# Moving sums to GpSimd and re-ordering the v stage of a hybrid RG-LRU and gated-MLP block on Trainium2

## The chip, the cores and the metric

The kernel runs on one core of one Trainium2 chip. The metric is the device time of one execution in microseconds. Five engines matter: TensorE (PE) multiplies matrices, VectorE (DVE), ScalarE (ACT) and GpSimd (POOL) work elementwise, and SyncE (SP) issues nearly all DMAs. Each engine runs its own instructions in order and waits on semaphores for the others.

## What is computed

One decoder block on x of 1024 tokens by 1024 channels, float32. The part that matters here is the first half, cut from the reference:

```
h = rms_norm(x, norm_mix_g)
rnn_x, rnn_gate, sgu_u, sgu_v, gate_a, gate_b = split(h @ w_in)
y_a = gelu(rnn_gate) * rg_lru(conv(rnn_x))        # decays use softplus(-rg_lambda)
v = layer_norm(gelu(sgu_v))                       # over 1024 channels, per token
mixed = einsum(tril(w_s), v) + b_s                # within chunks of 128 tokens, 8 groups
y_b = gelu(sgu_u) * mixed
merged = sigmoid(gate_a) * (y_a @ w_proj_a) + sigmoid(gate_b) * (y_b @ w_proj_b)
x = x + merged @ w_out
```

A SwiGLU channel mixer and a final RMSNorm follow. The change does not touch them.

## The kernel before

**Precision.** Each float32 operand is split into a high half, rounded on ACT, and a low half, subtracted on DVE (`split`, L91 to L94). A product is three matmuls: high by high, high by low, low by high (`mm3`, L96 to L99). For weights the pair of halves is made by `split_w`.

**The v stage** (pool `phv`, from L462). Tokens are rows here, in eight tiles t of 128. A first pass computes the first 512 channels of v for all tiles (product pv0, weight wv0), a second pass the other 512 (pv1, weight wv1; the loop at L708). After a tile's second half its statistics are complete: `v_stats` (gelu, bn_stats, bn_aggr), `v_norm` (the scale, by `rstd_early`, a chain of tiny instructions of one or two columns; tiles 1 and 2, 3 and 4, 5 and 6 share one chain), `v_centre` (four ACT instructions for a pair of tiles). One or two tiles later `v_split` makes the halves vn of v times its scale, ACT the high and DVE the low one, `v_mix` multiplies them on PE with the masked w_s (product mx), ACT copies one part (tile mt) and `v_mixed` adds the other on DVE and stores the sum to `mix_d`. The iteration of tile t mixes tile t - 2.

**Left operands.** From the u pair on, the input projections are done as 2x2 Strassen-Winograd products, seven instead of eight: M1 to M7 with left operands A11, A12, S4, A22, S1, S2, S3 (`LEFT`). They are made from the normalized x of the two halves of tokens F[0] and F[1]. `scale_x` normalizes a piece on DVE; `sums(i)` and `sum_s4(i)` (L548 to L555) make S1 to S4 in place, for the two halves i of the channels; `part` splits one half of an operand. The right operands need differences of weight blocks: `sums13` and `sum2` (L194 to L205).

**The order of the work.** Everything from L564 to the end of the u pair's first products (L787) stands in a hand-written order: within `tc.manual_schedule` each of the five engines issues its instructions in the order of the program text. Work behind it is ordered by the framework and may be issued between these instructions. Weights go through one queue of loads and splits: `weight` splits what a product needs and `ahead` more entries, `pump` splits up to a given entry. In the u pair (u0 and u1, order M1, M2, M5, M6, M3, M7, M4), `head` issues the next product, and `take` the evacuations that were postponed.

**Buffers.** vn has two, mt four, and S1's sums one (tag `shift`), so the sums of half 1 wait until the split of S1's half 0 has been done. The PSUM has eight banks.

**Recurrence constants.** softplus of lam is made after the u pair: lam is loaded by SP, ACT does Abs and Exp, and DVE does 17 instructions on 128x8 (L876 to L892).

## Time and profile before

| | |
|---|---|
| median of three runs | 1421.23 us (1419.32 to 1421.56) |
| the profiled execution | 1423.84 us |
| its span, first to last instruction | 1422.1 us |
| PE busy | 1399.9 us, 98% |
| PE weight loads busy | 1152.5 us, 81% |
| DVE busy | 1099.4 us, 77% |
| ACT busy | 793.3 us, 56% |
| POOL busy | 75.0 us, 5% |
| mean granted PE clock over the span | 0.996 |

All times within the execution are counted from the start of the span. The profiled execution took 1.7 us more than its span. Busy shares are means over stages with different limits. Matmuls are pipelined, so a PE that is always busy is not shown to be at its peak. In a timeline row the number in brackets is the idle time of that engine just before the instruction, with what ended it. PEclk is the clock that was granted to TensorE, as a share of its full 2.4 GHz.

The v stage's second pass runs from about 54 to 111 us, the u pair's products from 114 to 164 us, and the channel mixer, the only place where POOL does sums in this kernel, from about 800 to 1210 us.

### The profile page before, as it was taken

The page shows a single profiled execution, that of the slowest core. Times are in us where ns is not written, and L with a number is a line of the kernel's source. Part 1 is how long each engine was busy: PE and PEld are TensorE (multiplying, and loading weights), DVE is VectorE, ACT ScalarE, POOL GpSimd, SP SyncE. Part 2 cuts the span into 40 slices and gives each one's busy share as a digit, 9 for nine tenths or more (in the row PEclk, how much of TensorE's full clock was granted, in tenths as well). Part 3 has the DMA queues.
Part 4 walks back from the last instruction along what each step waited for, and adds up shares of the span by engine and source line. Part 5 has one row for each costly group of instructions (what it writes and reads, how often), then busy time and mean ns, then how long its engine had stood idle before and what let it go on. Part 6 is the DMA issues. An engine that isn't in the chain of part 4 may idle for free.

```text
span 1422.1 us, 17200 instructions
## 1 busy us (share of the span) xinstructions
PE 1399.9 (98%) x6216; PEld 1152.5 (81%) x6216; DVE 1099.4 (77%) x1807; ACT 793.3 (56%) x1320; POOL 75.0 (5%) x59
## 2 busy tenths in 40 slices
PE   9999999999999999999999999999999999999997
PEld 7877787788888887888888788888888888888886
DVE  6988999988888877788756976666666664697585
ACT  8567688888889865453543543333333333444454
POOL 0000000000000000000000021111111111000000
PEclk9999999999999999999999999999999999999999
DMA  9323645533333388683611133332232226852342
GB/s 322 138 60 101 196 169 171 175 125 104 116 108 114 104 303 320 236 322 127 230 60 45 74 112 112 111 112 91 102 112 112 111 85 256 331 191 85 112 141 81
DMA packets 72197, 212.45 MB, mean 149 GB/s; under 512 B 6448, under 2 KB 20784, under 8 KB 59568
## 3 DMA queue, kind: packets, MB, share of 16 engines
q1 hardware_dynamic: 71968, 211.32, 41.7%
q8 instruction: 48, 0.79, 0.2%
q14 instruction: 37, 0.30, 0.1%
q10 hardware_dynamic: 144, 0.04, 0.0%
HBM read 148.68 MB, written 62.65 MB: 149 GB/s over the span
## 4 chain that ended last, share of the span: by engine, by line
PE 74%; DVE 13%; ACT 8%; DMA 2%; issue 2%; SPq 0%; POOL 0%; DVEq 0%; ACTq 0%; POOLq 0%
PE f_p L97 10%; PE f_p L99 10%; PE f_p L98 10%; PE d_M L99 5%; PE d_M L97 5%; PE d_M L98 5%; PE g_p L98 2%; PE g_p L97 2%; PE g_p L99 2%; PE pb_p L97 2%; PE pb_p L99 2%; PE pb_p L98 2%; PE po L99 2%; PE po L97 2%; PE po L98 2%
## 5 line engine op out<-in xcount | busy, mean ns | idle before, releaser
L93 ACT ACTIVATE dl_M<-wraw 128x512 fp32r<-128x512 f32 x77 | 48.6, 631 | 104.9 <-PE d_M L99 92.3
L98 PE MATMUL d_M<-d_M,dl_M 128*128 128x512 f32 x264 | 102.8, 389 | 0.0
L97 PE MATMUL d_M<-d_M,dl_M 128*128 128x512 f32 x264 | 102.7, 389 | 0.0
L99 PE MATMUL d_M<-d_M,dl_M 128*128 128x512 f32 x264 | 102.7, 389 | 0.0
L93 ACT ACTIVATE f_t<-wraw 128x512 fp32r<-128x512 f32 x88 | 55.2, 630 | 84.1 <-PE f_p L99 64.1
L94 DVE TENSOR_TENSOR dl_M<-wraw,dl_M 128x512 fp32r<-128x512 f32 x77 | 54.0, 701 | 51.6 <-ACT dl_M L93 51.3
L94 DVE TENSOR_TENSOR f_t<-wraw,f_t 128x512 fp32r<-128x512 f32 x88 | 70.8, 806 | 23.4 <-ACT f_t L93 22.4
L97 PE MATMUL f_p<-f_S,f_t 128*128 128x512 f32 x176 | 68.6, 390 | 0.3 <-ACT f_t L93 0.3
L97 PE MATMUL f_p<-m,f_b 128*128 128x512 f32 x176 | 68.6, 390 | 0.0
L98 PE MATMUL f_p<-f_S,f_t 128*128 128x512 f32 x176 | 68.5, 389 | 0.0
L99 PE MATMUL f_p<-m,f_b 128*128 128x512 f32 x176 | 68.5, 389 | 0.0
L98 PE MATMUL f_p<-m,f_t 128*128 128x512 f32 x176 | 68.5, 389 | 0.0
L99 PE MATMUL f_p<-m,f_t 128*128 128x512 f32 x176 | 68.5, 389 | 0.0
L98 PE MATMUL f_p<-m,f_b 128*128 128x512 f32 x176 | 68.5, 389 | 0.0
L99 PE MATMUL f_p<-f_S,f_t 128*128 128x512 f32 x176 | 68.4, 390 | 0.0
L97 PE MATMUL f_p<-m,f_t 128*128 128x512 f32 x176 | 68.3, 389 | 0.0
L94 DVE TENSOR_TENSOR f_b<-wraw,f_b 128x512 fp32r<-128x512 f32 x66 | 47.2, 719 | 15.6 <-ACT f_b L93 14.9
L93 ACT ACTIVATE f_b<-wraw 128x512 fp32r<-128x512 f32 x66 | 40.9, 625 | 32.4 <-PE f_p L99 29.9
L98 PEld LDWEIGHTS d_M<-d_M,dl_M 128*128 128x128 f32 x264 | 49.6, 188 | 10.5 <-DVE d_M L94 0.2
L99 PEld LDWEIGHTS d_M<-d_M,dl_M 128*128 128x128 f32 x264 | 49.5, 188 | 10.3
L97 PEld LDWEIGHTS d_M<-d_M,dl_M 128*128 128x128 f32 x264 | 49.5, 188 | 10.2
L198 DVE TENSOR_TENSOR wraw<-wraw 128x512 f32<-128x512 f32 x50 | 53.0, 1060 | 1.1
(506 smaller groups left out, 4212.9 us busy)
## 6 DMA issues: line engine op xcount, KB each, us to landing
wraw<-in_w_gu_dram SPq DMA_DIRECT2D x22, 1024.0 KB, 4.9
wd<-in_w_down_dram SPq DMA_DIRECT2D x11, 1024.0 KB, 9.6
wraw<-in_w_r_dram SPq DMA_DIRECT2D x8, 1024.0 KB, 7.0
wraw<-in_w_g_dram SPq DMA_DIRECT2D x8, 1024.0 KB, 5.0
wraw<-ffs_d SPq DMA_DIRECT2D x8, 1024.0 KB, 5.0
wraw<-ffa_d SPq DMA_DIRECT2D x6, 1024.0 KB, 6.1
xn<-in_x_dram SPq DMA_DIRECT2D x8, 512.0 KB, 9.3
wraw<-in_w_u_dram SPq DMA_DIRECT2D x4, 1024.0 KB, 5.1
```

The source lines that it names most:

```text
L93: act.activation(hi, src, AF.Copy)
L94: return (eng or dve).tensor_sub(lo, src, hi.bitcast(F32))
L97: pe.matmul(o, lh, rh, start=start, stop=False, **kw)
L98: pe.matmul(o, lh, rl, start=False, stop=False, **kw)
L99: pe.matmul(o, ll, rh, start=False, stop=stop, **kw)
L198: dve.tensor_sub(raw[:, 0], raw[:, 2], raw[:, 0])
```

## The change

`sums` and `sum_s4` go from DVE to POOL, and so do `sums13` and `sum2` for u0 and u1 (the split of b22 inside `sum2` stays on ACT and DVE). The parts of the left operands move: A11's two halves to tiles 0 and 1, the first sums to tile 1, A12 to tile 5, S1's second half to tile 6. `v_mixed` becomes `mix_out(t, q)`, with one tile and one store for two mixing products; for the last two tiles it takes the places of v. In tile 7's iteration the first u weight is split, tile 5 is mixed and tile 6's vn made ahead of tile 7's statistics. In the u pair nothing is split ahead by the queue itself, but by explicit `pump` calls; the S3 and A22 parts and M3 move into the hand-written order. The constants of the recurrence are computed near the start: lam is loaded from ACT's queue, Abs and Exp are ACT's first instructions, and DVE's part stands before the first `x_rms`.

```diff
--- before.py
+++ after.py
@@ -191,18 +191,18 @@
     NORMED = ("M1", "M2", "M6", "M5", "M7", "M3", "M4")
     cur, postponed = {"misc": None, "defer": False}, []
 
-    def sums13(name, raw):
+    def sums13(name, raw, eng=dve):
 
         if (name, "t1") not in ready:
             ready[(name, "t1")] = True
-            dve.tensor_sub(raw[:, 0], raw[:, 2], raw[:, 0])
-            dve.tensor_sub(raw[:, 2], raw[:, 3], raw[:, 2])
-
-    def sum2(name, raw):
+            eng.tensor_sub(raw[:, 0], raw[:, 2], raw[:, 0])
+            eng.tensor_sub(raw[:, 2], raw[:, 3], raw[:, 2])
+
+    def sum2(name, raw, eng=dve):
 
         if (name, "b22") not in ready:
             ready[(name, "b22")] = split_w(raw[:, 3], f"{name}_b22")
-            dve.tensor_sub(raw[:, 3], raw[:, 3], raw[:, 0])
+            eng.tensor_sub(raw[:, 3], raw[:, 3], raw[:, 0])
 
     def plan(names, srcs, order=STEADY):
         lds = [new_load(s) for s in srcs]
@@ -374,7 +374,28 @@
     ident = const.tile([P, P], F32, name="ident")
     dve.memset(eps_t, EPS)
     make_identity(nc, ident)
-    act.activation(small.tile([P, 1], F32, name="warm", bufs=1), eps_t, AF.Gelu_apprx_tanh)
+    lam = const.tile([P, 8], F32, name="lam")
+    lam_c = const.tile([P, 2, 8], F32, name="lam_c")
+    act.dma_start(pv, a["pv"])
+    act.dma_start(lam, a["lam"])
+
+    def recurrence_constants(wk):
+
+
+        sp = {n: wk.tile([P, 8], F32, name=f"sp_{n}") for n in ("z", "z2", "p")}
+        e = lam_c[:, 0]
+        dve.tensor_scalar(sp["z"], e, 2.0, None, ALU.add)
+        dve.reciprocal(sp["z"], sp["z"])
+        dve.tensor_mul(sp["z"], sp["z"], e)
+        dve.tensor_mul(sp["z2"], sp["z"], sp["z"])
+        dve.tensor_scalar(sp["p"], sp["z2"], 1.0 / 17, None, ALU.mult)
+        for c in (15, 13, 11, 9, 7, 5, 3):
+            dve.scalar_tensor_tensor(sp["p"], sp["p"], 1.0 / c, sp["z2"], ALU.add, ALU.mult)
+        dve.scalar_tensor_tensor(sp["p"], sp["p"], 1.0, sp["z"], ALU.add, ALU.mult)
+        dve.tensor_scalar(sp["z"], lam, -1.0, 0.0, ALU.mult, ALU.max)
+        dve.scalar_tensor_tensor(sp["p"], sp["p"], 2.0, sp["z"], ALU.mult, ALU.add)
+        dve.tensor_scalar(lam_c[:, 0], sp["p"], RG_C / 2, None, ALU.mult)
+        dve.tensor_scalar(lam_c[:, 1], sp["p"], -RG_C, None, ALU.mult)
 
     def par(name, f):
         o = PV[name][0] + f
@@ -545,14 +566,15 @@
         def block(h, kh, i):
             return F[h][:, 4 * kh + 2 * i:4 * kh + 2 * i + 2]
 
+
         def sums(i):
             s1 = s1s[i] = wk.tile([P, 2, HALF], F32, name=f"xs{i}", tag="shift")
-            dve.tensor_add(s1, block(1, 0, i), block(1, 1, i))
-            dve.tensor_sub(block(1, 0, i), block(0, 0, i), block(1, 0, i))
-            dve.tensor_sub(block(0, 0, i), s1, block(0, 0, i))
+            pool.tensor_add(s1, block(1, 0, i), block(1, 1, i))
+            pool.tensor_sub(block(1, 0, i), block(0, 0, i), block(1, 0, i))
+            pool.tensor_sub(block(0, 0, i), s1, block(0, 0, i))
 
         def sum_s4(i):
-            dve.tensor_sub(block(0, 1, i), block(0, 1, i), block(0, 0, i))
+            pool.tensor_sub(block(0, 1, i), block(0, 1, i), block(0, 0, i))
 
         sts = {}
 
@@ -564,7 +586,10 @@
         ms = tc.manual_schedule(engines={mybir.EngineType.Pool, mybir.EngineType.Activation, mybir.EngineType.DVE,
                                          mybir.EngineType.PE, mybir.EngineType.SP})
         ms.__enter__()
-        act.dma_start(pv, a["pv"])
+
+        act.activation(lam_c[:, 0], lam, AF.Abs)
+        act.activation(lam_c[:, 0], lam_c[:, 0], AF.Exp, scale=-1.0)
+        act.activation(small.tile([P, 1], F32, name="warm", bufs=1), eps_t, AF.Gelu_apprx_tanh)
         first, second = slice(0, P), slice(P, 2 * P)
         xt_load(0, slice(0, 4), first)
         start_loads(1)
@@ -600,6 +625,7 @@
         squares(1)
         x_load(4)
         x_load(5)
+        recurrence_constants(wk)
         x_rms(0)
         x_split(2)
         x_diag(0)
@@ -677,64 +703,73 @@
                 for src in (v0[u], v1[u]):
                     act.activation(src, src, AF.Identity, bias=mvs[g[0]][:, 2, j:j + 1])
 
-        def v_split(t):
-            vn[t] = []
-            for q, src in enumerate((v0[t], v1[t])):
-                x = wk.tile([P, 2, HALF], F32R, name=f"vn{t}{q}", tag="vn", bufs=2)
-                act.activation(x[:, 0], src, AF.Identity, scale=stats[t])
-                dve.scalar_tensor_tensor(x[:, 1], src, stats[t], x[:, 0].bitcast(F32), ALU.mult, ALU.subtract)
-                vn[t].append(x)
+        def v_split(t, q):
+            x = wk.tile([P, 2, HALF], F32R, name=f"vn{t}{q}", tag="vn", bufs=2)
+            src = (v0, v1)[q][t]
+            act.activation(x[:, 0], src, AF.Identity, scale=stats[t])
+            dve.scalar_tensor_tensor(x[:, 1], src, stats[t], x[:, 0].bitcast(F32), ALU.mult, ALU.subtract)
+            vn[t, q] = x
 
         def v_mix(t):
-            mts[t] = []
+
             for i in range(4):
                 g = 2 * i
-                x = vn[t][i // 2]
-                mx = ps(f"mx{t}{i}").rearrange("p (j s t) -> p j s t", j=2, s=2)
+                x = vn[t, i // 2]
+                mx = mts[t, i] = ps(f"mx{t}{i}").rearrange("p (j s t) -> p j s t", j=2, s=2)
                 for j in range(2):
                     c = ts((g + j) % 4)
                     pe.matmul(mx[:, j], x[:, 0, c], ws[:, g + j], start=True, stop=False, skip_group_check=True)
                     pe.matmul(mx[:, j, 0], x[:, 1, c], ws[:, g + j, 0], start=False, stop=True, skip_group_check=True)
-                mt = wk.tile([P, 2, P], F32, name=f"mt{t}{i}", tag="mt", bufs=4)
-                act.activation(mt, mx[:, :, 1], AF.Copy)
-                mts[t].append((mt, mx))
-
-        def v_mixed(t):
-            for i, (mt, mx) in enumerate(mts.pop(t)):
-                g = 2 * i
-                dve.tensor_add(mt, mt, mx[:, :, 0])
-                nc.sync.dma_start(mix_d[i // 2][:, g % 4:g % 4 + 2, ts(t)], mt)
+
+        def mix_out(t, q):
+
+            if t < NT - 2:
+                m = wk.tile([P, 2, 2, P], F32, name=f"mt{t}{q}", tag="mt", bufs=2)
+            else:
+
+                m = wk.tile([P, HALF], F32, name=f"mt{t}{q}", tag="va", bufs=8).rearrange("p (i j t) -> p i j t", i=2, j=2)
+            for i in range(2):
+                act.activation(m[:, i], mts[t, 2 * q + i][:, :, 1], AF.Copy)
+            for i in range(2):
+                dve.tensor_add(m[:, i], m[:, i], mts.pop((t, 2 * q + i))[:, :, 0])
+            nc.sync.dma_start(mix_d[q][:, :, ts(t)], m.rearrange("p i j t -> p (i j) t"))
 
         for t in range(NT):
             acc = ps(f"pv1{t}")
             if t == 0:
                 state["limit"] = 2 * NK
-            tm_half(acc, "wv1", H, t, range(NK), free=2 * (t == NT - 1))
+            tm_half(acc, "wv1", H, t, range(NK))
             if t > 1:
-                v_split(t - 2)
+                for q in range(2):
+                    v_split(t - 2, q)
             if t < 2:
+                part("A11", block(0, 0, t), t)
                 scale_x(1, range(4 * t, 4 * t + 4))
-            if 1 <= t < 3:
-                part("A11", block(0, 0, t - 1), t - 1)
-            if t == 2:
+            if t == 1:
                 sums(0)
             if t == 4:
                 part("S1", s1s[0], 0)
                 sums(1)
             if t == 5:
+                for i in range(2):
+                    part("A12", block(0, 1, i), i)
+                sum_s4(0)
+            if t == 6:
                 part("S1", s1s[1], 1)
-                part("A12", block(0, 1, 0), 0)
-            if t == 6:
-                part("A12", block(0, 1, 1), 1)
-                sum_s4(0)
-            if t == 7:
                 sum_s4(1)
+            if t == NT - 1:
+                allow(2 * NK + 1)
+                v_mix(t - 2)
+                for q in range(2):
+                    mix_out(t - 2, q)
+                    v_split(t - 1, q)
             v_stats(t, acc)
             if t == group[t][-1]:
                 v_norm(t)
-            if t > 1:
+            if 1 < t < NT - 1:
                 v_mix(t - 2)
-                v_mixed(t - 2)
+                for q in range(2):
+                    mix_out(t - 2, q)
             if t == group[t][-1]:
                 v_centre(t)
             tick()
@@ -749,7 +784,8 @@
             return lambda c: res[n][i](c) if n in res else results.append(lambda: res[n][i](c))
 
         U = {n: wino(n, ops, *(call(n, i) for i in range(4)), order=LATE) for n in ("u0", "u1")}
-        state["ahead"] = 3
+        raw = {n: loads[queue[where[(n, "M1")]][0]][2] for n in U}
+        state["ahead"] = 0
 
         def head(n):
             next(U[n])
@@ -761,30 +797,51 @@
             del postponed[:n]
 
         cur["defer"] = True
-        v_split(6)
         head("u0")
+        pump(where["u1", "M2"] + 1)
+        sums13("u0", raw["u0"], pool)
+        sums13("u1", raw["u1"], pool)
         v_mix(6)
-        v_mixed(6)
-        v_split(7)
+        for q in range(2):
+            v_split(7, q)
+            mix_out(6, q)
+        for n in U:
+            sum2(n, raw[n], pool)
         head("u1")
         take(2)
         head("u0")
+        pump(where["u1", "M5"] + 1)
         v_mix(7)
-        v_mixed(7)
-        part("S2", block(0, 0, 0), 0)
+        for q in range(2):
+            mix_out(7, q)
         head("u1")
-        part("S2", block(0, 0, 1), 1)
+        for i in range(2):
+            part("S2", block(0, 0, i), i)
+        pump(where["u1", "M6"] + 1)
+        head("u0")
         take(2)
+        head("u1")
+        take(2)
+        for i in range(2):
+            part("S4", block(0, 1, i), i)
         head("u0")
         head("u1")
-        part("S4", block(0, 1, 0), 0)
+        state["ahead"] = 5
+        head("u0")
         take(2)
-        part("S4", block(0, 1, 1), 1)
-        head("u0")
+        a22 = [wk.tile([P, 2, HALF], F32, name=f"a22_{i}", tag="vn", bufs=2) for i in range(2)]
+        for i in range(2):
+            part("S3", block(1, 0, i), i)
+        for i in range(2):
+            act.activation(a22[i], block(1, 1, i), AF.Copy)
         head("u1")
-        take(2)
+        for i in range(2):
+            part("A22", a22[i], i)
         cur["defer"] = False
     ms.__exit__(None, None, None)
+    for fn in postponed:
+        fn()
+    postponed.clear()
 
     with tc.tile_pool(name="phr", bufs=2) as wk:
 
@@ -860,36 +917,8 @@
         for fn in results:
             fn()
         results.clear()
-        for i in range(2):
-            part("S3", block(1, 0, i), i)
-        for i in range(2):
-            c = wk.tile([P, 2, HALF], F32, name=f"a22_{i}", tag="rr")
-            act.activation(c, block(1, 1, i), AF.Copy)
-            s1s[i] = c
-        for i in range(2):
-            part("A22", s1s[i], i)
-        state["ahead"] = 5
         run(U["u0"], U["u1"])
 
-
-
-        lam = wk.tile([P, 8], F32, name="lam", bufs=1)
-        load(lam, a["lam"])
-        sp = {n: wk.tile([P, 8], F32, name=f"sp_{n}", bufs=1) for n in ("e", "z", "z2", "p", "m", "c4", "c8")}
-        act.activation(sp["e"], lam, AF.Abs)
-        act.activation(sp["e"], sp["e"], AF.Exp, scale=-1.0)
-        dve.tensor_scalar(sp["z"], sp["e"], 2.0, None, ALU.add)
-        dve.reciprocal(sp["z"], sp["z"])
-        dve.tensor_mul(sp["z"], sp["z"], sp["e"])
-        dve.tensor_mul(sp["z2"], sp["z"], sp["z"])
-        dve.tensor_scalar(sp["p"], sp["z2"], 1.0 / 17, None, ALU.mult)
-        for c in (15, 13, 11, 9, 7, 5, 3):
-            dve.scalar_tensor_tensor(sp["p"], sp["p"], 1.0 / c, sp["z2"], ALU.add, ALU.mult)
-        dve.scalar_tensor_tensor(sp["p"], sp["p"], 1.0, sp["z"], ALU.add, ALU.mult)
-        dve.tensor_scalar(sp["m"], lam, -1.0, 0.0, ALU.mult, ALU.max)
-        dve.scalar_tensor_tensor(sp["p"], sp["p"], 2.0, sp["m"], ALU.mult, ALU.add)
-        dve.tensor_scalar(sp["c4"], sp["p"], RG_C / 2, None, ALU.mult)
-        dve.tensor_scalar(sp["c8"], sp["p"], -RG_C, None, ALU.mult)
 
         def gate_pair(f):
             kept = []
@@ -954,8 +983,8 @@
             def decays():
                 for h in range(2):
                     q[h] = wk.tile([P, HALF], F32, name=f"th{f}{h}", tag="th")
-                    act.activation(q[h], r[h], AF.Tanh, scale=sp["c4"][:, f:f + 1])
-                    act.activation(r[h], r[h], AF.Exp, scale=sp["c8"][:, f:f + 1])
+                    act.activation(q[h], r[h], AF.Tanh, scale=lam_c[:, 0, f:f + 1])
+                    act.activation(r[h], r[h], AF.Exp, scale=lam_c[:, 1, f:f + 1])
                     dve.tensor_mul(i[h], i[h], xc[h])
                 y_ahead(ya_d, "ya", f)
                 later(1, factors)
```

## Rows read from the trace of the kernel before

**Rows 1.** Windows of 10 us: length, busy us (instructions) per engine, PEclk, DMA share, GB/s.
```profile
70.00:80.00 10.00, 8.59 (x45) 6.91 (x43) 9.52 (x24) 5.75 (x12) 0.00 (x0) 1.00 0.05 13
...
120.00:130.00 10.00, 10.00 (x49) 8.60 (x48) 8.42 (x17) 5.93 (x14) 0.00 (x0) 0.83 0.20 58
...
140.00:150.00 10.00, 7.19 (x23) 5.17 (x23) 8.20 (x12) 7.95 (x13) 0.00 (x0) 0.83 0.35 106
...
160.00:170.00 10.00, 10.00 (x46) 8.29 (x45) 10.00 (x17) 5.10 (x10) 0.00 (x0) 1.00 0.74 251
```

**Rows 2.** PE's waits up to 260 us: us in total, times, longest us.
```profile
PE u_p L97 <- ACT u_t L93: 2.8, 1, 2.8
PE mx L696 <- ACT vn L684: 2.4, 2, 1.3
PE mx L697 <- DVE vn L685: 2.3, 4, 1.2
```

**Rows 3.** PE in order of time: start us, us, instruction, count [idle before, releaser].
```profile
54.48 0.50 PE L98 MATMUL pv<-wv,h 128*128 128x512 f32 x1
...
70.83 0.22 PE L697 MATMUL mx<-ws,vn 128*128 128x128 f32 x1
...
72.50 0.45 PE L97 MATMUL pv<-wv,h 128*128 128x512 f32 x1
...
79.50 0.39 PE L696 MATMUL mx<-ws,vn 128*128 128x256 f32 x1 [1.29 <-ACT vn L684]
...
118.61 0.33 PE L697 MATMUL mx<-ws,vn 128*128 128x128 f32 x1 [1.23 <-DVE vn L685]
...
121.20 0.63 PE L98 MATMUL u_p<-h_A,u_b 128*128 128x512 f32 x1
```

**Rows 4.** DVE in order of time, v stage, tiles 1 and 2.
```profile
64.42 2.71 DVE L515 SCALAR_TENSOR_TENSOR x<-x,pv,rms 128x512 f32<-128x512 f32 x4
...
69.03 0.70 DVE L685 SCALAR_TENSOR_TENSOR vn<-va,rv,vn 128x512 fp32r<-128x512 f32 x1
...
71.44 1.22 DVE L550 TENSOR_TENSOR xs<-x 128x1024 f32<-128x1024 f32 x1
...
76.54 0.16 DVE L407 TENSOR_TENSOR rv<-rv 128x2 f32<-128x2 f32 x1
```

**Rows 5.** ACT in order of time, where lam is read.
```profile
140.95 0.21 ACT L879 ACTIVATE sp_e<-lam 128x8 f32<-128x8 f32 x1 [1.76 <-DMA lam<-in_lam_dram]
141.17 1.28 ACT L880 ACT_TABLE_LOAD   x1
```

**Rows 6.** ACT in order of time, first stage.
```profile
16.74 3.31 ACT L484 ACTIVATE h<-x,pv 128x256 fp32r<-128x256 f32 x8 [1.64 <-DMA x<-in_xt_dram]
```

**Rows 7.** DVE in order of time: first scales, second weight's halves, the constants' chain.
```profile
22.16 0.17 DVE L400 TENSOR_SCALAR rx<-ssqs 128x2 f32<-128x2 f32 x1 [1.59 <-ACT xn L488]
...
29.47 0.17 DVE L400 TENSOR_SCALAR rx<-ssqs 128x2 f32<-128x2 f32 x1 [0.26 <-ACT xn L488]
...
53.76 4.88 DVE L94 TENSOR_TENSOR wv<-wraw,wv 128x512 fp32r<-128x512 f32 x8
...
174.32 0.77 DVE L887 SCALAR_TENSOR_TENSOR sp_p<-sp_p,sp_z 128x8 f32<-128x8 f32 x4
```

**Rows 8.** GpSimd (POOL) in order of time, channel mixer.
```profile
864.32 1.62 POOL L1217 TENSOR_TENSOR ff1s<-ff1s,ff1a 128x512 f32<-128x512 f32 x1
...
1207.04 1.29 POOL L1217 TENSOR_TENSOR ff10s<-ff10s,ff10a 128x512 f32<-128x512 f32 x1
```

**Rows 9.** DVE in order of time, channel mixer.
```profile
845.78 0.69 DVE L199 TENSOR_TENSOR wraw<-wraw 128x512 f32<-128x512 f32 x1
...
863.12 1.67 DVE L198 TENSOR_TENSOR wraw<-wraw 128x512 f32<-128x512 f32 x1
864.83 1.67 DVE L199 TENSOR_TENSOR wraw<-wraw 128x512 f32<-128x512 f32 x1
```

**Rows 10.** ACT in order of time, centring of tile 7.
```profile
115.00 0.72 ACT L678 ACTIVATE va<-va,mv 128x512 f32<-128x512 f32 x1 [0.45 <-DVE mv L669]
```

## The prediction

> **What bounds the kernel now.** I read four views in this order. The page has TensorE (PE) busy nearly throughout, so what can be won is what PE waits for, plus what it does at the lower clock. The windows of 10 us place both: between 70 and 150 us, in the v stage and the first half of the u pair, PE is not full in several windows, and the granted clock is 0.83 in two of them [rows 1]. The list of PE's waits up to 260 us names what it waited for: ScalarE (ACT) and VectorE (DVE) halves of the normalized v (vn), 2.4 and 2.3 us, and one weight half of the u pair, 2.8 us [rows 2]. PE's order in time places these: 1.29 and 0.43 at the mixing of tile 1, as much again (1.53) at the mixing of tile 3, 0.21 and 1.23 about tiles 5 and 6, then the 2.8; behind the last two the products are spaced as in the row of 0.63 us, which is the lower level, 1.2 instead of 2.4 GHz [rows 3]. A mean of 0.83 over 10 us is 3.4 us at half rate, so 1.7 us lost, twice [rows 1].
>
> What the change can remove is therefore 2.4 + 2.3 + 2.8 of waits and 3.4 of slow clock: 10.9 us of 1421. I look at whether it removes these, and what it puts there.
>
> **Why these waits exist.** DVE's order has three left-operand sums of 1.22 us (L550 to L552) ahead of the statistics of the same tile. The statistics end in a chain of nine tiny instructions of 0.16 us which gives the scale; ACT needs that for vn [rows 4]. So 3.7 us of sums delay the chain at tiles 2 and 4, and PE waits at the next mixing. The 2.8 us has another source: ACT waits for lam, then loads a table, before it can split the weight half [rows 5].
>
> **lam and its table load leave the u pair.** ACT was idle 1.76 us for lam, then spent 0.21, 1.28 and 0.21 us [rows 5]. All that goes: the 2.8 us wait is gone and the 1.7 us of slow clock behind it. Gain 4.5. Late next is the half itself, whose raw weight is in SBUF by then, so nothing follows.
>
> **The same work at t = 0.** On ACT it is two activations of 0.21 us and one more load of 1.28, behind a small transfer. ACT waits 1.64 us for x at 16.74 [rows 6], so a delay of some 1.3 us at the start is gone by then. On DVE, 17 instructions of eight columns stand ahead of the first scales. Four dependent ones took 0.77, so 14 of these take 2.7 and three independent ones 0.3: 3.0 us. DVE had 1.59 us idle at that place and 0.26 before the next scales [rows 7]; from there to the second weight's halves at 53.76 I find no gap that is not itself a wait for the scales. PE's product at 54.48 waits for the first of those halves (0.50 instead of 0.39) [rows 3, 7]. So 1.2 us comes out there. Bounds: 0, if the 0.5 us gaps of the later scale chains give way, and 1.8, if the 0.26 does not. PE arriving late from the start would wait anyway, so the larger of the two counts.
>
> **The sums on GpSimd.** Eight of 1.22 and six weight differences of 0.69 leave DVE, 13.9 us. The trace has no 1024-column subtraction on GpSimd. The nearest rows are those of 512 columns: 1.29 us with DVE idle. The one at 864.32 took 1.62 beside a DVE subtraction that ran from 863.12 to 864.79; if it could not begin its own work before that, 1.15 is left for it [rows 8, 9]. Twice that, less one start (0.1), is 2.2; twice 1.29 is 2.6. I take 2.3, nearer the row with DVE at work, as here.
>
> The same rows show the price that matters: DVE's subtraction of 845.78 took 0.69, the one that began at 864.83 took 1.67. It ended 0.56 after GpSimd's (865.94). So the two engines take turns: each instruction waits out the other's. On a full queue a DVE instruction that reads two tensors in SBUF loses up to 2.3 us, even one of 0.16 us. That the short ones and those with a scalar are held as well I infer; no row shows it. The Trainium skill, "SBUF — State Buffer", section "Who interferes with whom", says it outright: a DVE instruction with two SBUF inputs contends with a GpSimd instruction that reads SBUF, and the second is blocked for all of the first. By that rule the first rival below falls away and the sum stays as it is; the subtractions' rows agree (1.67 for 0.69).
>
> Now place by place, on PE's time:
> - *Mixing of tile 0.* Before, DVE split vn at 69.03, and PE took the first half at 70.83 without a wait [rows 3, 4]. Now both A11 halves (1.22 each) stand ahead of DVE's scalings of x, which push vn to about 71.0 (one was there, one is new, and the second waits 0.7 for ACT). The first sum starts when six of eight scalings are done, about 69, and holds the first vn half until 71.3; it is ready at 72, a wait of 1.1. Then the second sum has the turn until 74.2, and the second half is ready at 75, where PE wanted it 2.0 earlier. New: 3.1. Bounds: 0.8 (DVE held by nothing) and 3.7 (sums of 2.6).
> - *Mixing of tile 1.* The scale chain now waits only for the rest of the third sum, 1 us instead of 3.7, and PE comes 3 us later. The 1.72 goes.
> - *Mixing of tile 3.* The sums of the second half wait for the S1 part, which reads the buffer they write, and so lie beside tile 4's statistics. The chain's first instruction waits out the second sum (0.9), its second the third (2.3): 3.2 us, where the sums themselves stood for 3.7. PE arrives without the earlier wait. So 1.8 for the 1.53 that goes. Bounds 0 and 2.8.
> - *Mixing of tile 4.* Two S4 sums beside its vn halves: 0.5, bounds 0 and 1.1.
> - *u1's first product.* Mixing of tile 6 no longer waits, since its halves are made inside tile 7's pass: the 1.44 goes. But u1's weight split now stands on ACT behind tile 7's centring (two of 0.72 [rows 10]), which waits for DVE, which has two mixings' additions, two vn halves and one turn of GpSimd (1.1) first. ACT has the weight about 7 us after tile 7's last matmul by this order alone, and 1.1 more by the turn, while PE wants it after mixing, product, mixing: 1.8 + 2.7 + 1.8 (a mixing is 70.8 to 72.5 and its first instruction; a product is twelve matmuls, of which a full window holds 46) [rows 1, 3]. With DVE's half, 2.2. Bounds 1.0 and 2.4.
>
> The mixing's stores (sixteen on SP's queue for thirty-two, nothing behind them that PE needs here) and the S3 and A22 parts, moved ahead, lie beside a PE that the last window shows full [rows 1]. If that cover went, the parts' halves of 1.22 on DVE would show.
>
> **Slow clock after the change.** Waits of 1.23 and of 2.8 were followed by the lower level, the pair 1.29 + 0.43 was not [rows 1, 3]. The wait before u1's product stands where the 1.23 stood, and is longer, so 1.7 there. The one at tile 0 comes in two parts with matmuls between, like the pair: 0, bound 1.7.
>
> **Sum.** Removed 10.9. Added 1.2 + 3.1 + 1.8 + 0.5 + 2.2 + 1.7 = 10.5. Net -0.4: the profiled execution of 1423.84 would become 1423.4. It stands 2.6 above the median of 1421.23; there it is 1420.8.
>
> **Rivals.**
> *DVE's short instructions and those with a scalar are not held* (faster). For it: only 512-column subtractions are shown to be held. Against: the reason can hardly be the length. Left are 1.2 at the start, 0.8 at tile 0, 1.1 before u1 and one slow stretch of 1.7: 4.8 against 10.9, so -6.1: 1415.1; without the slow stretch 1413.4.
> *The sums cost the upper bound* (slower). Place: the scale chain of tile 4 and the halves of tiles 0 and 4. Price 2.6 per sum: waits 3.7 + 2.8 + 1.1 + 2.2, with 1.2 and slow clock twice 14.4 against 10.9: +3.5, 1424.7. It decides from about 2.5 us per sum on. For it: GpSimd starts each with a fixed part, and with DVE idle 512 columns took 1.29. Against: 1.15 in turns. A page's figure bears on this alone: the Trainium skill, "GPSIMD Engine Reference", section "Elementwise — side-by-side cycle accounting", gives 4.5 us for 2048 columns, hence as an estimate 2.25 here; the sum by it would be -0.8, and no row has this size.
>
> **Chances.** 0.2% is 2.8 us, about what a measurement of this kernel can tell from no change: faster is below 1418.4, slower above 1424.1. Forecast 0.46, own range 1417 to 1425 (0.07 faster, 0.34 same, 0.05 slower). First rival 0.29, all faster. Second 0.25 (0.20 slower, 0.05 same). Sums: 0.36, 0.39, 0.25. The range runs from the first rival without its slow stretch to the second with 1.3 more at the start: 1413.5 to 1426.
>
> **What would show it.** DVE's vn instructions of 1.5 to 3 us instead of 0.74 at tile 0, and tiny ones of over 1 us at tile 4, bear out the turns; GpSimd's sums of 2.2 to 2.4 us the price. PE's waits should be at the mixings of tiles 0 and 3 and before u1, with none at tile 1 and none of 2.8 in the u pair. The product at 54.48 should come 1.2 later. Wrong would be: vn at 0.74 beside a running sum, or no wait at tile 0.

## The result and the profile after

The changed kernel took 1429.25 us, the median of five executions (1429.22 to 1432.17), beside 1421.56 us of the kernel before (1419.32 to 1423.74): a ratio of 1.0059, 95% interval 1.0048 to 1.0069. It is slower by 0.6%, and 3 us above the end of the range. Its profiled execution took 1430.05 us, with a span of 1428.3.

Windows of 10 us of the kernel after (columns as in [rows 1]):

```profile
70.00:80.00 10.00, 7.44 (x40) 6.06 (x39) 9.55 (x22) 4.71 (x10) 7.30 (x3) 1.00 0.00 0
100.00:110.00 10.00, 9.54 (x45) 8.43 (x46) 9.97 (x13) 6.12 (x11) 6.12 (x2) 0.83 0.35 107
120.00:130.00 10.00, 8.82 (x46) 7.15 (x45) 9.36 (x22) 7.96 (x17) 3.31 (x2) 1.00 0.16 49
140.00:150.00 10.00, 10.00 (x46) 8.29 (x45) 7.11 (x10) 5.28 (x8) 0.00 (x0) 1.00 0.00 0
160.00:170.00 10.00, 10.00 (x46) 8.27 (x45) 7.89 (x13) 3.84 (x8) 0.10 (x1) 1.00 0.59 186
170.00:180.00 10.00, 7.07 (x31) 5.00 (x29) 9.93 (x17) 2.50 (x4) 0.00 (x0) 1.00 0.85 290
```

The window of 140 to 150, where lam was waited for, is full now and at the higher clock. A new hole stands at 170 to 180, behind the stage that the prediction looked at: PE is without work for 2.9 us while DVE is full. PE's timeline of the kernel after names the waits in order:

```profile
72.49 0.33 PE L722 MATMUL mx<-ws,vn 128*128 128x128 f32 x1 [0.98 <-DVE vn L710]
...
75.26 0.33 PE L722 MATMUL mx<-ws,vn 128*128 128x128 f32 x1 [1.57 <-DVE vn L710]
...
99.28 0.39 PE L721 MATMUL mx<-ws,vn 128*128 128x256 f32 x1 [2.80 <-ACT vn L709]
...
100.46 0.33 PE L722 MATMUL mx<-ws,vn 128*128 128x128 f32 x1 [0.79 <-DVE vn L710]
...
124.45 0.50 PE L97 MATMUL u_p<-h_A,u_b 128*128 128x512 f32 x1 [1.18 <-ACT u_b L93]
...
136.12 0.50 PE L97 MATMUL u_p<-h_S,u_t 128*128 128x512 f32 x1 [1.03 <-DVE mt L734]
...
171.79 0.50 PE L99 MATMUL r_p<-h_A,r_b 128*128 128x512 f32 x1 [1.10 <-DVE r_b L94]
...
176.20 0.50 PE L97 MATMUL r_p<-h_S,r_t 128*128 128x512 f32 x1 [1.83 <-ACT r_y L243]
```

Up to 165 us these are the places of the forecast, but for the wait at 136.12, which it did not list. The recurrence's products take over from the u pair at 164.85 us, after 164.29 before: 0.6 us later. The second recurrence pair begins at 210.33 after 205.23, the fourth at 296.53 after 289.69. PE in the kernel after, then in the kernel before:

```profile
164.85 0.39 PE L98 MATMUL r_p<-h_A,r_b 128*128 128x512 f32 x1
...
210.33 0.39 PE L97 MATMUL r_p<-h_A,r_b 128*128 128x512 f32 x1
```

```profile
164.29 0.39 PE L97 MATMUL r_p<-h_A,r_b 128*128 128x512 f32 x1
...
205.23 0.39 PE L97 MATMUL r_p<-h_A,r_b 128*128 128x512 f32 x1
```

So most of the loss is made past the u pair. Times taken from two traces are not exact to the microsecond: the profiled execution before stands 2.3 us above its median and that after 0.8, and one product of the v stage that stands at 54.96 us here comes at 55.97 in the first run below, whose code is the same up to there.

### The profile page after: what moved, and what is told of

Same layout as the page of the kernel before. It is cut to its first block, busy times and chain, and to the rows that moved or that the text cites. A ratio compares the mean times of both kernels' runs of the same rounds, so it can differ in the third digit from the quotient of the medians.

```text
span 1428.3 us, 17154 instructions
## 1 busy us (share of the span) xinstructions
PE 1398.3 (98%) x6216; PEld 1150.9 (81%) x6216; DVE 1103.8 (77%) x1793; ACT 792.8 (56%) x1321; POOL 105.8 (7%) x73
## 4 chain that ended last, share of the span: by engine, by line
PE 72%; DVE 15%; ACT 8%; issue 2%; DMA 1%; SPq 0%; ACTq 0%; DVEq 0%
PE f_p L97 9%; PE f_p L99 9%; PE f_p L98 9%; PE d_M L99 5%; PE d_M L97 5%; PE d_M L98 5%; PE g_p L98 2%; PE g_p L99 2%; PE g_p L97 2%; PE pb_p L97 2%; PE pb_p L99 2%; PE pa_p L99 2%; PE pa_p L97 2%; PE pb_p L98 2%; PE pa_p L98 2%
```

## The experiments

Three parts of the change can be had one by one: the constants at t = 0; the sums on GpSimd (eight in the v stage, six weight differences in the u pair); the new order, whose *end* (the products M3, called third products in the expectations, S3 and A22 parts, copies of A22, all within the hand-written order) is kept apart. All ratios are to the kernel before, run beside them, with their 95% intervals. The rows that begin with "new order" have the constants too, and all sums on DVE where nothing else is said. The "first run" is that of the first row.

| kernel | median us | ratio |
|---|---|---|
| change without the end (first run) | 1427.2 | 1.0036 (1.0023 to 1.0049) |
| change, A22 alone behind | 1428.4 | 1.0051 (1.0038 to 1.0064) |
| change, all sums on DVE | 1429.5 | 1.0056 (1.0044 to 1.0068) |
| constants alone | 1419.8 | 0.9987 (0.9978 to 0.9995) |
| constants, v sums on GpSimd | 1424.1 | 1.0019 (1.0010 to 1.0028) |
| constants, new order | 1420.4 | 0.9992 (0.9983 to 1.0001) |
| constants, end of the order | 1425.7 | 1.0028 (1.0016 to 1.0039) |
| first run, u pair as before | 1425.3 | 1.0023 (1.0013 to 1.0032) |
| new order, split early | 1418.4 | 0.9977 (0.9968 to 0.9985) |
| new order, split early, sums late | 1416.8 | 0.9970 (0.9959 to 0.9981) |
| new order, split early, sums later | 1416.6 | 0.9966 (0.9953 to 0.9978) |
| new order, sums late on GpSimd | 1420.6 | 0.9997 (0.9988 to 1.0006) |
| new order, end without A22 | 1422.8 | 1.0006 (0.9997 to 1.0015) |
| new order, differences on GpSimd | 1424.4 | 1.0020 (1.0012 to 1.0029) |

**The end of the order put back.**

```diff
         head("u0")
         head("u1")
-        state["ahead"] = 5
-        head("u0")
         take(2)
-        a22 = [wk.tile([P, 2, HALF], F32, name=f"a22_{i}", tag="vn", bufs=2) for i in range(2)]
-        for i in range(2):
-            part("S3", block(1, 0, i), i)
...
         results.clear()
+        for i in range(2):
+            part("S3", block(1, 0, i), i)
...
```

> The changed kernel with only the end of the hand-written order put back: the third products of the u pair, the S3 and A22 parts and the copies of A22 stand behind that order again, in the next pool's places, as in the kernel before. Theory A (the loss is made by this end of the order: the u pair's outputs are held back past it, and their VectorE work falls into the first recurrence pair): the products of the recurrence pairs come 6 us or more earlier against the changed kernel, time 1421 to 1424 us. Rival B (the loss comes from GpSimd's sums and the moved mixing, and only shows late): the time stays at 1427 to 1430. Rival C (from the constants at t = 0): also 1427 to 1430.

1427.2 us: 2 us off, not 6, and so in the range of rivals B and C. The loss behind 165 us is gone all the same, as two windows show, of 35 and of 135 us (columns as in [rows 1]). The kernel before:

```profile
130.00:165.00 35.00, 32.19 (x134) 25.82 (x134) 31.35 (x44) 25.09 (x37) 0.10 (x1) 0.95 0.53 175
165.00:300.00 135.00, 133.37 (x584) 108.95 (x583) 126.89 (x218) 106.42 (x159) 0.30 (x3) 1.00 0.51 171
```

The kernel after:

```profile
130.00:165.00 35.00, 33.41 (x153) 26.95 (x152) 29.05 (x40) 24.01 (x39) 3.49 (x3) 1.00 0.33 108
165.00:300.00 135.00, 127.75 (x556) 103.28 (x555) 125.85 (x201) 104.11 (x152) 0.31 (x3) 1.00 0.56 188
```

With the end put back:

```profile
130.00:165.00 35.00, 31.53 (x144) 25.18 (x142) 33.50 (x49) 23.01 (x36) 3.49 (x3) 1.00 0.58 186
165.00:300.00 135.00, 133.59 (x582) 108.64 (x582) 124.28 (x200) 107.29 (x160) 0.30 (x3) 1.00 0.50 168
```

Past 165 us PE is idle for 7.3 us in the kernel after, 1.6 before, 1.4 here. From 130 to 165 it is the other way round: DVE idles for 6.0 us in the kernel after and 1.5 here, and PE waits 3.5 here against 1.6. The recurrence's first pair now begins at 167.95 us, 3 us later than in the kernel after, and the second at 209.41, only 0.9 earlier. Theory A has the place right, but something else uses up what it frees; the runs on GpSimd below show what.

**A22 alone behind**, S3 and the products M3 kept in the order.

```diff
-        a22 = [wk.tile([P, 2, HALF], F32, name=f"a22_{i}", tag="vn", bufs=2) for i in range(2)]
...
-        for i in range(2):
-            part("A22", a22[i], i)
...
+            c = wk.tile([P, 2, HALF], F32, name=f"a22_{i}", tag="rr")
+            act.activation(c, block(1, 1, i), AF.Copy)
...
```

> The changed kernel with only the copies of A22 and the A22 parts behind the hand-written order, in the next pool's places; S3's parts and the third products stay in it. Theory A in its first form (the next pool's tiles wait for the memory that the copies hold, so the mixing's loads start at 161 us): the loads start 8 us or more earlier, by about 152, behind the weight loads that stand before them, and half of the loss or more goes: 1422 to 1426 us. Theory A in its second form (it is the place in each engine's order, not the memory): the loads move, but the time stays within 1.5 us of the changed kernel, 1427.5 to 1430.

1428.4 us, the second form's range, and not to be told from the change itself (1.0038 to 1.0064 beside 1.0048 to 1.0069). The first load of a mixing moved from 161.27 to 140.99 us, so A22's copies were what held it. PE's hole moved too, into the u pair, where M7 now waits for S3, with a clock of 0.83 over 160 to 170 us behind it (this run's PE timeline):

```profile
157.74 0.73 PE L97 MATMUL u_p<-h_S,u_t 128*128 128x512 f32 x2 [2.54 <-ACT h_S L93]
```

**All sums back on DVE.** `pool` becomes `dve` in `sums`, `sum_s4` and the calls of `sums13` and `sum2`.

> The changed kernel with every sum and weight difference that it gave to GpSimd back on VectorE, at the same places in the order. Theory A: the recurrence's loss of 6 to 7 us stays; the v stage trades the 3.6 us of waits at tile 3's mixing for up to three pieces of 1.1 us each in VectorE's queue: 1426 to 1431 us. Rival B: with no GpSimd beside VectorE most of the loss goes, 1424 us or less.

1429.5 us, as theory A has it. Without GpSimd the hole past 165 us is even larger, 8.2 us of PE:

```profile
130.00:165.00 35.00, 33.72 (x151) 27.28 (x150) 28.98 (x42) 23.48 (x37) 0.10 (x1) 1.00 0.39 125
165.00:300.00 135.00, 126.83 (x544) 102.38 (x543) 124.00 (x198) 103.08 (x149) 0.30 (x3) 0.99 0.54 182
```

**Constants alone.** The kernel before with `lam`, `lam_c` and `recurrence_constants` as in the change.

> The kernel before with only the recurrence's constants moved to t = 0, everything else as it was. Theory A (this part is a gain of the change): the 2.8 us wait for lam and one slow stretch of the clock behind it go, 0.5 us at the first v1 product comes: 3 to 4 us faster, 1417 to 1419 us. Rival C (the constants cost at the start and the tables are loaded in a worse order): no faster than before, 1420.5 us or more.

1419.8 us, 1.9 us faster: between the two ranges, but its interval ends below 1, so rival C falls. In the window where lam was waited for PE has 8.79 us at full clock, after 7.19 at 0.83 [rows 1], so 3.3 us are won there, 1.6 of waiting and 1.7 of slow clock; PE still waits 0.73 and 0.47 for the weight halves behind. In the profiled execution a slow stretch has come up elsewhere, which takes some of it back: the clock is 0.83 over 80 to 90 us, behind the waits of 1.29 and 0.43 that tile 1 has here as before, where the kernel before had 1.00. The window in this run:

```profile
140.00:150.00 10.00, 8.79 (x38) 6.73 (x37) 9.99 (x14) 9.03 (x14) 0.00 (x0) 1.00 0.34 105
```

**The v stage's sums on GpSimd, at the places of before.**

```diff
-            dve.tensor_add(s1, block(1, 0, i), block(1, 1, i))
+            pool.tensor_add(s1, block(1, 0, i), block(1, 1, i))
...
```

> The kernel before with the constants at t = 0 and the eight sums of the v stage on GpSimd, at the places in the order that they have before (a sum per block after tiles 2, 4, 6 and 7); all else as before, so it is the constants-only kernel (1419.8 us) with one more part of the change. Theory G (GpSimd's pieces of 2.4 us hold VectorE's instructions, and this is what costs): slower than the constants alone by 2 us or more, 1421.8 to 1426. Theory D (it is the new order of parts, mixing and products that costs): within 1.5 us of the constants alone, 1418 to 1421.

1424.1 us: 4.4 more than the constants alone. Theory G holds. PE waits 1.11 and 1.58 at tile 0's mixing and 1.19 and 0.79 at tile 3's.

**Constants and the new order, without its end and without GpSimd.** The first run's kernel with `dve` in all sums.

> The changed kernel with the end of its order put back as before (as in the second of these runs' forerunners, 1427.2 us) and all of GpSimd's sums back on VectorE: what is left of the change is the constants and the new order of parts, mixing and products up to the sixth pair. Theory D: stays near 1427, 1425 to 1429. Theory G: most of the loss goes, 1419.5 to 1423.

1420.4 us: theory D falls. The new order's 0.6 us over the constants alone cannot be told from nothing (0.9983 to 1.0001 beside 0.9978 to 0.9995). So the first run's loss of 6.8 us over this kernel is GpSimd's. The one long wait left is 4.4 us at tile 0's mixing, with a clock of 0.83 over 70 to 90 us behind it; two of 1.01 and 1.25 us follow, before u1's first product and behind tile 7's mixing.

**The end of the order alone, with the constants.**

```diff
+        state["ahead"] = 5
+        head("u0")
         take(2)
+        a22 = [wk.tile([P, 2, HALF], F32, name=f"a22_{i}", tag="vn", bufs=2) for i in range(2)]
...
```

> The constants-only kernel (1419.8 us) with the end of the order of the changed kernel alone: third products, S3 and A22 parts and the copies of A22 in the hand-written order. Theory A (this end costs by itself, because the u pair's outputs wait behind it): 2 to 6 us slower than the constants alone, 1422 to 1426, with products of the first recurrence pair waiting for 3 us or more in 165 to 190 us. Otherwise (it costs only on top of a late VectorE): within 1 us of 1419.8.

1425.7 us: 5.9 more than the constants alone. The waits are not where the text put them: 0.66 us at 168.54, but 1.57 and 0.52 at 150 (S3's parts), 0.59 at 224, 2.42 at 266.

**The first run with the u pair's order and its weight differences as before.**

```diff
         head("u0")
-        pump(where["u1", "M2"] + 1)
-        sums13("u0", raw["u0"], pool)
-        sums13("u1", raw["u1"], pool)
...
```

> The kernel with the end of the order put back (1427.2 us), and now the whole order of the u pair's products as before too, with its weight differences on VectorE; the v loop keeps the sums on GpSimd, the spread parts and the new mixing. If the new order of the u pair costs (1.6 us at tile 7's mixing, 1.5 at the S part): 2 to 4 us less, 1423 to 1425. If the v loop costs alone: 1426 to 1428.

1425.3 us, 1.9 off, between the two ranges. The split of the first u weight is back at its old place as well. The run does not part order from GpSimd; the last run below does.

**Tile 0's operand made one tile earlier**, on the kernel with constants and new order.

```diff
-            if t > 1:
+            if t > 2:
                 for q in range(2):
                     v_split(t - 2, q)
+            if t == 1:
+                for q in range(2):
+                    v_split(0, q)
```

> The kernel with constants, new order and all sums on VectorE (1420.4 us), and tile 0's second left operand made one tile earlier, ahead of tile 1's part, scales and sums. If the 4.4 us wait at tile 0's mixing and the slow clock behind it (1.7 us) come from the three sums that the change moved from tile 2 to tile 1, ahead of that operand: the wait goes, tile 1's mixing, whose chain still stands behind the sums, waits 1 to 3.5 us: 1415 to 1419 us. If VectorE is the bound through this stage: the time stays within 1 us of 1420.4 and the wait shows elsewhere.

1418.4 us. Tile 0 waits no more; tile 1 waits 2.46 and 0.43 behind the sums. DVE was not the bound there.

**The first sums at tile 3 as well** (`if t == 3: sums(0)`).

> As the run before it, and the first three sums at tile 3, behind tile 1's operands, instead of tile 1. If the chains of tiles 0 and 1 are what the sums hold up: no wait over 1 us at the mixings of tiles 0 and 1, 4 to 6 us off 1420.4: 1414.5 to 1417. If VectorE is the bound: within 1 us of 1420.4.

1416.8 us: no wait at tiles 0 and 1; 1.90 and 0.44 at tile 3.

**The sums later still**: the first three at tile 4, the second three at tile 6, the S1 parts and the S4 sums behind them, and A11's second half at tile 3.

> As the second run of this call, with the sums still later: the first three at tile 4, the second three at tile 6, the parts behind them. Chains alone: as that run or up to 1.5 us less, 1413.5 to 1417; VectorE's backlog carried into the u pair: waits of 2 us or more there, 1417 to 1421.

1416.6 us. Both sides were partly right: 0.43 is left at the mixings, but u0's product waits 2.42 us for a weight half. It is the fastest kernel here, 0.34% below the kernel before, and cannot be told from the one ahead of it.

**The late sums on GpSimd** (`pool` in `sums` and `sum_s4`).

> As the second run of this call, with the eight sums on GpSimd. Theory G (GpSimd holds VectorE's instructions wherever its sums stand, and the chain of a later tile is always beside them): 2 to 6 us slower than that run. Otherwise (GpSimd cost the change only where the chains of tiles 0 and 4 stood beside it): within 1 us of it or faster, since VectorE loses eight pieces of 1.2 us.

1420.6 us, 3.7 more than on DVE. At late places too the chain of a tile stands beside them: 2.99 and 0.60 us at tile 3's mixing, 0.58 and 0.78 at tile 1's.

**The end without A22, no GpSimd.** The new order with the products M3 and S3's parts in it, A22 behind.

> The kernel with constants, new order and all sums on VectorE (1420.4 us; with the whole end of the changed kernel's order it took 1429.5), and of that end only the third products and the S3 parts; A22's copies and parts stay behind in the next pool's places. If the end costs because the u pair's outputs wait for the places of A22's copies: the mixing's loads start by 142 us, and most of the 9 us stays away, 1420 to 1423. If it costs by its place in the engines' order alone: 1426 to 1430.

1422.8 us instead of 1429.5 with A22: of the 9.1 us that the end costs without GpSimd (1429.5 against 1420.4), 6.7 go with A22's copies and parts. The first load of a mixing stands at 138.55 us. The windows of this run:

```profile
130.00:165.00 35.00, 32.27 (x146) 25.92 (x145) 33.35 (x51) 22.02 (x35) 0.10 (x1) 1.00 0.58 190
165.00:300.00 135.00, 133.98 (x587) 109.72 (x586) 126.09 (x202) 108.09 (x160) 0.30 (x3) 1.00 0.52 171
```

**Only the six weight differences on GpSimd**, new order, `pool` in the calls of `sums13` and `sum2`.

> The kernel with constants, new order and all sums on VectorE (1420.4 us), with only the u pair's six weight differences on GpSimd. If GpSimd's pieces cost in the u pair as they do in the v stage: 1 to 3 us slower, 1421.4 to 1423.4, with VectorE's instructions beside them at two to five times their length. If not: within 0.7 us, 1419.7 to 1421.1.

1424.4 us: 4.0 us, more than expected. Part of it may be the clock: in the profiled execution 0.83 over 150 to 160 us, and 1.00 in that of the kernel without it. Beside GpSimd two weight halves took 3.49 us on DVE, against 1.29 in the kernel without it; the backlog reaches S4's parts, and PE waits for them (this run's DVE and then PE timeline):

```profile
132.16 3.49 DVE L94 TENSOR_TENSOR u_t<-wraw,u_t 128x512 fp32r<-128x512 f32 x2
```

```profile
149.99 0.80 PE L98 MATMUL u_p<-h_S,u_b 128*128 128x512 f32 x1 [1.95 <-DVE h_S L94]
```

## Why the prediction was wrong

**The step that failed** first is the one costed at nothing: "The mixing's stores ... and the S3 and A22 parts, moved ahead, lie beside a PE that the last window shows full [rows 1]." It looked for cover on PE and priced the parts themselves. It did not ask what their memory holds up. A22's copies now take vn's places in the v stage's pool, and the pool behind it, whose tiles hold the u pair's outputs, reuses that memory. SyncE's waits in the kernel after, 110 to 190 us (us in total, times, longest):

```profile
SPq L467 <- DVE h_A L94: 9.1, 1, 9.1
```

This wait ends when DVE has split A22's second half (DVE and then SP's queue in the kernel after):

```profile
159.97 1.22 DVE L94 TENSOR_TENSOR h_A<-a,h_A 128x1024 fp32r<-128x1024 f32 x1
```

```profile
161.27 0.33 SPq L467 DMA_DIRECT2D mix<-mix_d  x1
```

In the kernel before this first load of a mixing stood at 133.64 us (SP's queue there):

```profile
133.64 0.33 SPq L446 DMA_DIRECT2D mix<-mix_d  x1
```

The 9.1 us are the last part of that delay. Ahead of them two weight loads, which stand behind the first loads of the mixing when A22 is out of the order, now come first in the queue, which stands 11.9 us until a buffer for the first of them is free. DVE, which before did the outputs' multiplications (L905 and L908 of the kernel after) from 139 us on, idled for 6 of the 35 us up to 165. Its first output then waited for these loads (DVE in the kernel after):

```profile
164.83 0.75 DVE L905 SCALAR_TENSOR_TENSOR mix<-mix,pv,sh 128x512 f32<-128x512 f32 x1 [1.11 <-DMA sh<-shift_d]
```

So it did them beside the first recurrence pair's weight halves, where it is full. ACT's evacuation of that pair needs a buffer that one of the outputs' differences frees (ACT's timeline of the kernel after):

```profile
175.55 0.60 ACT L243 ACTIVATE r_y<-r_p 128x512 f32<-128x512 f32 x1 [9.63 <-DVE yb_s L877]
```

That is PE's 1.83 us at 176.20. Without GpSimd the whole end costs 9.1 us, and 6.7 of them go when A22 alone is taken out of it. No run kept the copies in the order with memory of their own, so the price of their memory is not parted from the price of their places on ACT and DVE; the trace speaks for the memory, since the loads wait for it and DVE is idle meanwhile. The other 2.4 us go with S3's parts and M3 in the order.

In the changed kernel the same end costs only 2.1 us by the medians (1429.25 to 1427.2) and 3.3 by the ratios. The two costs do not add up: the end alone is 9.1, GpSimd alone 6.8, both together 8.9 us over the 1420.4 of the kernel without either. The traces suggest why, though no run tests it: the end also puts S3's and S4's parts ahead of the outputs on a DVE that GpSimd has made late, and so saves the 1.5 to 2 us of PE which the first run and the last lose at S4. Why the end also brings single waits of 2.4 us far behind, for xs (272.24 us in the kernel after, 265.90 with the constants and the end alone), stays open.

**A second term was too small**, and the end of the order hid it: the u pair's six weight differences. With the end put back the time is still 1427.2 us, where the sum has 1420.8, and the u pair ends at 167.95 us, 3.7 later than before. In the sum these differences stand only as one turn of GpSimd (1.1) ahead of u1's weight. By themselves they cost 4.0 us: DVE's weight halves wait for them, S4's parts come late, and PE waits for these, 1.95 us in the last run and 1.49 in the first.

**GpSimd.** The forecast had it as a loss at PE's waits, and it is one: 3.7 to 4.4 us for the eight sums, 4.0 for the six differences, 6.8 for both. The places, one by one, as measured in the kernel after:
- *Price of a sum:* 2.3 forecast, 2.40 beside short instructions of DVE, 2.68 and 2.72 beside its vn halves.
- *Tile 0:* 3.1 forecast, 2.55 measured, in two parts, with no slow clock behind, as said.
- *Tile 1:* no wait, as said.
- *Tile 3:* 1.8 forecast, bound 2.8; 3.6 measured. The chain was given two turns of GpSimd (0.9 and 2.3) and took three: 1.19, 2.39 and 2.24 in the rows below. The forecast let it begin in the second sum and counted nine instructions; of the three ahead of these, of one tensor and a scalar, two were held too, and the first of them already met the first sum.
- *Tile 4:* 0.5 forecast; a vn half of 2.88 at 106.07 us, but no wait of PE.
- *u1's first product:* 2.2 forecast, 1.18 measured; 1.03 more at 136.12, for tile 7's mixing, which the prediction did not list.
- *Slow clock:* one stretch forecast and one found, but at 100 to 110 us behind tile 3, not before u1. That the number agrees is luck, as the last section shows: like waits were followed by the lower level in one execution and not in another.

The timelines of DVE and then of GpSimd in the kernel after, at tile 0 and tile 4, show the turns:

```profile
72.36 2.84 DVE L710 SCALAR_TENSOR_TENSOR vn<-vb,rv,vn 128x512 fp32r<-128x512 f32 x1
75.13 0.68 DVE L685 BATCH_NORM_STATS2 st<-vb 128x6 f32<-128x512 f32 x1
...
90.89 1.19 DVE L695 TENSOR_SCALAR mv<-mv 128x2 f32<-128x2 f32 x1
...
92.18 2.39 DVE L422 TENSOR_SCALAR rv<-rv 128x2 int32<-128x2 int32 x1
...
94.80 2.24 DVE L429 TENSOR_TENSOR rv<-rv 128x2 f32<-128x2 f32 x1
```

```profile
71.97 2.68 POOL L573 TENSOR_TENSOR x<-x,x 128x1024 f32<-128x1024 f32 x1
74.73 2.72 POOL L574 TENSOR_TENSOR x<-xs,x 128x1024 f32<-128x1024 f32 x1
89.65 2.40 POOL L572 TENSOR_TENSOR xs<-x 128x1024 f32<-128x1024 f32 x1 [12.19 <-DVE h_S L94]
92.13 2.41 POOL L573 TENSOR_TENSOR x<-x,x 128x1024 f32<-128x1024 f32 x1
94.62 2.40 POOL L574 TENSOR_TENSOR x<-xs,x 128x1024 f32<-128x1024 f32 x1
```

**What was to be removed** went: the 2.8 us for lam and the slow clock behind it, and the old waits at tiles 1, 5 and 6. **The constants at t = 0** were forecast at 1.2 us; the product of 54.48 came at 54.96, and at 55.32 with the constants alone. By these terms the sum up to the end of the u pair came out: -0.4 forecast, +0.6 measured. That is luck in part. In the first run, with the same v stage and the same sums, it is +3.7: there the outputs' work stands on DVE ahead of that point again, and the price of the weight differences shows.

**The rivals.** The first, short instructions not held, falls by the row of 2.24 us. The second, sums at 2.6, is nearer, and its sign was right; but the loss was not there. That both had the u pair's end as the last place where anything can happen is the same omission as that of the forecast.

**The new order** was forecast only through its waits. With its sums on DVE it gives no gain, for one reason above all: the three sums were moved to tile 1, ahead of tile 0's operand. DVE in the kernel with constants and new order, all sums on DVE:

```profile
71.17 1.22 DVE L572 TENSOR_TENSOR xs<-x 128x1024 f32<-128x1024 f32 x1
...
75.67 0.70 DVE L710 SCALAR_TENSOR_TENSOR vn<-va,rv,vn 128x512 fp32r<-128x512 f32 x1
```

and PE in the same kernel:

```profile
76.42 0.47 PE L722 MATMUL mx<-ws,vn 128*128 128x128 f32 x1 [4.38 <-DVE vn L710]
```

With operand first and sums later the same work takes 1416.6 to 1416.8 us, about 5 us below the kernel before and 12.5 below the change.

## What to carry to other kernels

Work that is moved ahead of a pool's end holds the pool's memory: look up whose first tiles, and whose DMAs in an in-order queue, wait for it, not only what lies beside it. A sum given to GpSimd is not off a busy VectorE; price it by the longest chain of instructions beside it that can be held, those of two tensors in SBUF and those of one tensor and a scalar, turn by turn, before counting what VectorE saves. Where a chain of tiny instructions sets the end, put it ahead of the bulk work on the same engine first: here that was worth 3.6 us (1420.4 to 1416.8), and the other engine lost time at each place where it was tried. When one step of a forecast fails, put it back and see whether the rest then holds: here it did not.

## What the runs showed of the hardware

VectorE's instructions of one tensor and a scalar on 128x2 elements were held like those of two tensors: L422 took 2.39 us beside a sum (0.17 at 77.59, without one), and L695 1.19. Not held were the statistics of one tensor (0.68 us at 75.13, beside the sum of 74.73) and the additions that read PSUM (four in 1.37 us at 104.11, beside the sums that run from 102.28 to 108.40). The Trainium skill, "SBUF — State Buffer", section "Who interferes with whom", has both: one-input instructions keep clear of GpSimd, except those, tensor_scalar among them, that can enter a mode which uses the shared ports. These rows agree with it.

In the kernel after the clock fell to 0.83 over ten us behind waits of 2.80 and 0.79, and not behind 0.98 and 1.57 at tile 0, nor behind the 1.18 before u1 (1.00 from 120 to 130), though 1.23 had been followed by it in the kernel before [rows 1, 3]. The length of the waits does not settle it. In the run with A22 alone behind, whose code is the same up to there, 1.02 and 1.58 at tile 0 went with a clock of 0.73 over 70 to 80 us; and with the constants alone 1.29 and 0.43 at tile 1, followed by 1.00 in the kernel before, were followed by 0.83.
